# A four-layer decoder trunk on one core: later OUT turns, even blocks first in the out projection, own banks for the last piece

## The chip, the cores and the metric

The kernel runs on one core of a Trainium2 chip. The metric is the device time of one execution in microseconds. A core has a matrix engine (PE, TensorE), a vector engine (DVE), a scalar engine (ACT), a general engine (POOL) and a queue engine (SP) that issues most of the DMAs. Each engine runs its own program in order and waits for the others by semaphores. PE writes its products into PSUM, eight banks of 128 x 512 floats; DVE and ACT read them from there.

## The reference, cut to what matters

Four layers work on one residual stream of 256 tokens by 1024 features. Each layer is a token mixer and a squared-ReLU MLP, both behind an RMS norm. Mixer 0 (layers 0 and 3) is differential attention, mixer 1 (layer 1) block-sparse attention, mixer 2 (layer 2) sliding-window attention with sinks.

```python
def rms_norm(x, g):
    return x * rsqrt(mean(x * x, -1) + 1e-6) * g

def diff_attention(h, w_in, w_out, lam, sub_g, cos, sin, lambda_init):   # 8 heads, two maps each
    q, k, v = split(h @ w_in)                  # 1024 each; rotary on the first quarter of each head
    p = softmax(causal(q @ k.T / 8))
    p = p[:, :, 0] - lam * p[:, :, 1]
    o = rms_norm(p @ v, sub_g) * (1.0 - lambda_init)
    return o.reshape(B, S, 1024) @ w_out

for i in range(4):
    a = rms_norm(h, attn_norm_g[i])
    h = h + (diff_attention, moba_attention, swa_sink_attention)[i % 3](a, ...)
    a = maximum(rms_norm(h, mlp_norm_g[i]) @ mlp_w_up[i], 0)      # 1024 x 4096
    h = h + (a * a) @ mlp_w_down[i]                               # 4096 x 1024
return rms_norm(h, final_norm_g)
```

## The kernel before, in words

All is float32. A product is made of rounded parts: each operand x is split into hi, x rounded to a shorter float that PE takes at full rate, and lo, the rest. `mm3` (lines 271 to 273) sums hi·hi, hi·lo and lo·hi; `block_step` (603, 604) does the same for tokens in the free dimension, with hi and lo of the tokens side by side in one 512-wide matmul and one 256-wide one.

**Weights.** They lie in DRAM as 128 x 2048 pieces in the order of use. `fetch` loads a piece into one of four raw buffers; `stage` (lines 80, 81) splits it in two halves of 1024 columns, `whi` on ACT and `wlo` on DVE, into one of three buffers each. `take` hands out the next piece and, before that, has the pieces up to two ahead staged. With three buffers, the piece two ahead takes the buffer of the piece last used, so its first `whi` waits until PE has done the last matmul that reads it.

**The residual stream** stands transposed in four tiles `hT0` to `hT3`, each with two blocks of 128 features by 256 tokens. `into` (line 622) adds the eviction of block d to its half of `hT`, and then calls `norm_part`, which makes the scaled hi and lo of the block for the next projection (`hg`, line 228 on ACT and 229 on DVE), and for each second block the squares for the norm (233, 238).

**A differential layer.** `proj` (296) computes six pieces of q, k and v, 512 columns each, and between them calls turns from a written `plan`: `QK` transposes q and k of a pair of heads (`p_qk`, 459), `SC` scores and softmax (`p_s`, 271 to 273), `TR` transposes the weights (`p_t`, 351, evicted as `et`, 352), `AV` multiplies by v (`p_av`, 357 to 359) and makes the normed output `o` of a pair of heads (404), and `OUT` transposes it (`p_o`, 409) and evicts hi and lo as `oo` (411, 412). `OUT(g)` yields the two heads of pair g, which group g of the out projection reads as `parts[2g]` and `parts[2g+1]`. Evicted projections are `qk` (586), followed by the rotary sums (304 to 309).

**The out projection.** `out_proj_all` (layers 0, 2, 3) keeps four PSUM banks `p_d0` to `p_d3`, two blocks of 256 columns in each. For each of four groups it takes one weight piece and adds, for the eight blocks in order, two heads by `mm3`: 48 matmuls per group. In the last group each block goes through `into` as soon as it is done. `out_proj` does layer 1.

**The MLP.** `up_proj` has 16 groups of two blocks; in the first group its eight steps run over both blocks together, so step k needs only `hg` of block k. In layer 3 a callback after the second group transposes the residual back to rows (`p_res`, 797). `down_proj` returns to the transposed stream; in the last layer `down_out` computes rows instead, in two pieces of 512 columns for each of two groups of 128 rows: `last` accumulates in a bank `p_last`, `close` adds the residual (`res`, 702) and squares it (704), `sofar` and `finish` make the norm's factor (710 to 717), scale the rows (719, 722) and write them out. The very last piece is done in two halves of 256 columns.

**Start.** `WARM` products of two 128 x 128 tiles (line 133, 2 passes each) run while the first data comes in.

The order of calls is not the order of each engine's program: a scheduler places the instructions of every engine when the kernel is built, and from then on each engine takes them in that order.

Of the kernel before, what the change touches and what calls it, by code (L numbers as in the profile page):

```python
# [11 lines left out]
F32 = mybir.dt.float32  # L12
F32R = mybir.dt.float32r
I32 = mybir.dt.int32
AF = mybir.ActivationFunctionType
OP = mybir.AluOpType
AX = mybir.AxisListType

P = 128
# [8 lines left out]
NEG = -1.0e38  # L28
LOOK = 2
FAR = 5  # L30
WARM = 11
RAW = 4


# [5 lines left out]
def trunk(ctx: ExitStack, tc: tile.TileContext, xT, gains, lams, swa_row, fng, weights, out):  # L40
# [8 lines left out]
    def bank(tag, name):  # L49
        return ps.tile([P, 512], F32, tag=tag, name=name, bufs=4)  # L50
# [427 lines left out]
    def mixer_layer(i, n):  # L478
        mixer, slot = i % 3, i // 3
        r = norm_factor(n)  # L480
        parts = []
# [43 lines left out]
        else:  # L525
# [43 lines left out]
                    [(TR, 4), (QK, 3), (OUT, 1), (SC, 6)], [(TR, 5), (SC, 7)],  # L569
                    [(AV, 4), (TR, 6), (AV, 5), (TR, 7), (AV, 6), (OUT, 2), (AV, 7), (OUT, 3)]]  # L570
            if mixer == 0:
                plan[8:] = [[(AV, 2), (QK, 2), (OUT, 0), (SC, 4)], [(AV, 3), (SC, 5)], [(TR, 4), (AV, 4), (OUT, 1)],
                            [(TR, 5), (AV, 5)],
                            [(QK, 3), (SC, 6), (SC, 7), (OUT, 2), (TR, 6), (AV, 6), (TR, 7), (AV, 7), (OUT, 3)]]
            for at, c in enumerate(order):
                p = proj(n, (512, 2), at == 0, [lambda do=do, x=x: do(x) for do, x in plan[2 * at]])
                if i == 0 and at == 0:
# [11 lines left out]
                    do(x)  # L589
            for do, x in plan[-1]:  # L590
                do(x)
            return parts
        for do in first + second:
            do()
        for _ in range(3):
            step()
        line.clear()
        return parts

# [22 lines left out]
        if b:  # L624
            norm_sum(n, j)

    def out_proj_all(parts, n):

        banks = [bank("acc", f"p_d{j}") for j in range(4)]
        for g in range(4):  # L630
            hi, lo = (r3(2)(x) for x in take())
            for d in range(8):
                p = banks[d // 2][:, S * (d % 2):S * (d % 2) + S]
                w = slice(P * d, P * d + P)
                for a in range(2):
                    x = parts[2 * g + a]
                    mm3(p, hi[:, a, w], lo[:, a, w], x[:, 0], x[:, 1], g + a + d % 2 == 0, g + a == 4,
                        skip_group_check=True)
                if g == 3:
                    into(n, d, p, None, True)  # L640

    def out_proj(parts, n):

        banks = [bank("acc", f"p_d{j}") for j in range(4)]
        two = [[r3(4)(x) for x in take()] for _ in range(2)]
        order = [(k, d) for k in range(6) for d in range(4)] + [(k, d) for d in range(4) for k in (6, 7)]
        for k, d in order:
            hi, lo = (x[:, k % 4, P * d:P * d + P] for x in two[k // 4])
            block_step(banks[d], hi, lo, parts[k], k == 0, k == 7)
            if k == 7:  # L650
                into(n, d, banks[d], None)
        for j in range(2):
            hi, lo = (r3(8)(x) for x in take())
            for b in range(2):
                p = bank("acc", f"p_e{b}")
                for k in range(8):
                    block_step(p, hi[:, k, P * b:P * b + P], lo[:, k, P * b:P * b + P], parts[k], k == 0, k == 7)
                into(n, 4 + 2 * j + b, p, None)
# [32 lines left out]
    def down_out(us, res, factor):  # L691

        grow = sb.tile([P, D], F32, tag="raw", name="grow", bufs=RAW)
        nc.sync.dma_start(grow, bcast(fng, D))
        ss = cst.tile([P, 4, NT], F32, name="fss")
        x = cst.tile([P, 2, NT], F32, name="fx")
        r = cst.tile([P, NT], F32, name="fr")

        def close(t, bank, c, part, first, width):

            y = res[t][:, 512 * c + first:512 * c + first + width]
            V.scalar_tensor_tensor(y, bank[:, first:first + width], factor[:, t:t + 1], y, op0=OP.mult, op1=OP.add)
            sq = sb.tile([P, 512], F32, tag="relu", name="sq")
            A.activation(sq[:, :width], y, AF.Square, accum_out=ss[:, part, t:t + 1])

        def finish(t, halves):

            o = slice(t, t + 1)
            last = x[:, 1, o]
            V.scalar_tensor_tensor(last, ss[:, halves, o], 0.5 / D, x[:, 0, o], op0=OP.mult, op1=OP.add)  # L710
            y, w = r[:, o], tiny.tile([P, 1], F32, tag="nw", name="nw", bufs=6)

            V.tensor_scalar(y.bitcast(I32), last.bitcast(I32), -0.5, 1597463007.0 - 2.0 ** 22 - 2.0 ** 31,
                            op0=OP.mult, op1=OP.add)
            for _ in range(3):
                V.scalar_tensor_tensor(w, y, y, last, op0=OP.mult, op1=OP.mult)
                V.scalar_tensor_tensor(y, w, 1.5, y, op0=OP.subtract, op1=OP.mult)
            rows = slice(P * t, P * t + P)
            A.activation(res[t][:, :512], res[t][:, :512], AF.Copy, scale=y)
            nc.scalar.dma_start(out[rows, :512], res[t][:, :512])  # L720
            for z in (slice(512, 768), slice(768, 1024)):
                V.scalar_tensor_tensor(res[t][:, z], res[t][:, z], y, grow[:, z], op0=OP.mult, op1=OP.mult)
                nc.sync.dma_start(out[rows, z], res[t][:, z])

        def sofar(t, parts):
            o = slice(t, t + 1)
            V.tensor_scalar(x[:, 0, o], ss[:, 0, o], 0.5 / D, 0.5 * EPS, op0=OP.mult, op1=OP.add)
            for j in parts:
                V.scalar_tensor_tensor(x[:, 0, o], ss[:, j, o], 0.5 / D, x[:, 0, o], op0=OP.mult, op1=OP.add)

        for c in range(2):
            banks = [bank("acc", "p_last") for _ in range(NT)]
            parts = []

            def last(t, ks, cols=slice(0, 512)):
                for q, k in ks:
                    hi, lo = parts[q]
                    u, s = us[4 * q + k], slice(P * t, P * t + P)
                    mm3(banks[t][:, cols], u[:, 0, s], u[:, 1, s], hi[:, k, cols], lo[:, k, cols],
                        q + k == 0, q + k == 10, skip_group_check=True)  # L740

            for q in range(8):
                parts.append([r3(4)(x) for x in take()])
                if q < 6:
                    for k in range(4):
                        for t in range(NT):
                            last(t, [(q, k)])
            ends = [(q, k) for q in (6, 7) for k in range(4)]
            last(0, ends)
            close(0, banks[0], c, c, 0, 512)  # L750
            if c == 0:
                last(1, ends)
                close(1, banks[1], 0, 0, 0, 512)
                for t in range(NT):
                    y = res[t][:, :512]
                    V.tensor_tensor(y, y, grow[:, :512], op=OP.mult)
                    sofar(t, [])
            else:
                finish(0, 1)
                last(1, ends[:4])  # L760
                for h in range(2):
                    last(1, ends[4:], slice(256 * h, 256 * h + 256))
                    close(1, banks[1], 1, 1 + h, 256 * h, 256)
                    if h == 0:
                        sofar(1, [1])
                finish(1, 2)
# [7 lines left out]
    for j in range(4):  # L774
        norm_sum(n, j)
    for i in range(DEPTH):
        parts = mixer_layer(i, n)
        n = new_norm(gv[:, 1, i, :])
        (out_proj if i % 3 == 1 else out_proj_all)(parts, n)
        held = {}  # L780

        def then(g):
            if i + 1 < DEPTH:
                if g == 1:
                    x = mean_row(n)
                    held["row"] = sb.tile([P, S], F32, tag="row", name="row", bufs=1)
                    V.reciprocal(held["row"], x)
            elif g == 1:
                held["factor"] = cst.tile([P, NT], F32, name="factor")
                V.reciprocal(held["factor"], mean_square(n))  # L790

                held["res"] = [room(16 + t, [P, D], f"res{t}") for t in range(NT)]
                for j in range(4):
                    p = bank("acc", "p_res")
                    for t in range(NT):
                        for b in range(2):
                            T.transpose(p[:, S * t + P * b:S * t + P * b + P],
                                        hT[j][:, S * b + P * t:S * b + P * t + P], ident)
                    for t in range(NT):
                        A.activation(held["res"][t][:, S * j:S * j + S], p[:, S * t:S * t + S], AF.Copy)  # L800

        us = up_proj(n, then)
        if i + 1 < DEPTH:
            n = new_norm(gv[:, 0, i + 1, :])
            down_proj(us, n, held["row"])
        else:
            down_out(us, held["res"], held["factor"])
# [78 lines left out]
```

## Time and profile before

| | us |
|---|---|
| median of 3 runs | 1155.39 (1154.45 to 1156.26) |
| profiled execution, its time | 1154.87 |
| its span | 1152.8 |
| PE busy | 1140.4 (99%) |
| DVE busy | 824.3 (72%) |
| ACT busy | 671.6 (58%) |

The span runs from the first to the last instruction of the profiled execution. In the timeline a row gives start, duration, engine, line, operation, output and inputs, shapes and count, and in brackets how long the engine was idle before and what released it. Matmuls overlap, so the distance from one start to the next is what one costs on PE; a matmul's own duration is longer. The waits are listed as total, times and longest.

### The profile page before, as it was taken

To read this page: it belongs to the slowest core of one execution; us is meant where nothing else is said; L and a number is where in the kernel's file an instruction comes from. 1 tells how busy PE (TensorE), PEld (TensorE's weight loads), DVE (VectorE), ACT (ScalarE), POOL (GpSimd) and SP (SyncE) were. 2 spreads that over 40 slices of the span, in tenths; PEclk is the share of its full clock that TensorE was granted. 3 is DMA by queue.
4 is the path that set the end of the run, shared out by engine and by line. 5 is a ranking of instruction groups with operands and counts; after the bars stand their busy time and mean duration, and the time that the engine had idled before them with its cause. 6 is when DMAs were issued, how large, how long until landed. Compare 5 with 4: busy or idle time off the path is not lost.

```text
span 1152.8 us, 17102 instructions
## 1 busy us (share of the span) xinstructions
PE 1140.4 (99%) x6558; PEld 986.6 (86%) x6558; DVE 824.3 (72%) x1631; ACT 671.6 (58%) x1239; POOL 11.4 (1%) x39
## 2 busy tenths in 40 slices
PE   9999999999999999999999999999999999999997
PEld 7789888888887888888898888888888889888886
DVE  8978977656666698775568787775567788777453
ACT  6866655544476765654447866654447676665342
POOL 1000000000000000000000000000000000000000
PEclk9999999999999999999999999999999999999999
DMA  8543455555544355555564246555553434554551
GB/s 327 194 146 119 160 200 193 199 190 183 183 146 145 116 178 193 200 192 183 185 209 142 74 147 206 195 184 186 184 201 129 152 136 155 194 199 166 186 179 36
DMA packets 30608, 198.66 MB, mean 172 GB/s; under 512 B 3520, under 2 KB 5184, under 8 KB 7360
## 3 DMA queue, kind: packets, MB, share of 16 engines
q1 hardware_dynamic: 30240, 197.06, 49.6%
q8 instruction: 51, 0.84, 0.3%
q10 hardware_dynamic: 288, 0.52, 0.1%
q14 instruction: 29, 0.24, 0.1%
HBM read 196.52 MB, written 1.05 MB: 171 GB/s over the span
## 4 chain that ended last, share of the span: by engine, by line
PE 92%; DVE 3%; ACT 2%; DMA 2%; issue 1%; SPq 0%; DVEq 0%; ACTq 0%
PE p_up L603 20%; PE p_in L296 16%; PE p_down L603 15%; PE p_up L604 10%; PE p_down L604 8%; PE p_last L271 2%; PE p_last L273 2%; PE p_last L272 2%; PE p_d L273 2%; PE p_d L271 2%; DMA raw<-in_weights 2%; PE p_d L272 2%; PE p_av L434 1%; PE p_t L351 1%; PE p_s L271 1%; PE p_qk L459 1%
## 5 line engine op out<-in xcount | busy, mean ns | idle before, releaser
L81 DVE TENSOR_TENSOR wlo<-raw,whi 128x1024 fp32r<-128x1024 f32 (+1 forms) x374 | 447.1, 1209 | 202.9 <-ACT whi L80 201.9
L80 ACT ACTIVATE whi<-raw 128x1024 fp32r<-128x1024 f32 (+1 forms) x374 | 384.7, 1045 | 210.1 <-issue 111.1
L603 PE MATMUL p_up<-hg,whi 128*128 128x512 f32 x1024 | 356.9, 393 | 0.5 <-DVE hg L229 0.2
L604 PE MATMUL p_up<-hg,wlo 128*128 128x256 f32 x1024 | 284.9, 279 | 0.0
L603 PE MATMUL p_down<-uu,whi 128*128 128x512 f32 x768 | 266.4, 392 | 0.0
L603 PEld LDWEIGHTS p_up<-hg,whi 128*128 128x128 f32 x1024 | 191.5, 187 | 43.3 <-DVE hg L229 0.7
L604 PE MATMUL p_down<-uu,wlo 128*128 128x256 f32 x768 | 214.3, 279 | 0.0
L296 PE MATMUL p_in<-whi,hg 128*128 128x512 f32 (+1 forms) x736 | 212.9, 372 | 0.1
L604 PEld LDWEIGHTS p_up<-hg,wlo 128*128 128x128 f32 x1024 | 193.2, 189 | 0.5
L603 PEld LDWEIGHTS p_down<-uu,whi 128*128 128x128 f32 x768 | 143.7, 187 | 32.1
L296 PEld LDWEIGHTS p_in<-whi,hg 128*128 128x128 f32 x736 | 131.8, 188 | 24.7 <-issue 1.2
L604 PEld LDWEIGHTS p_down<-uu,wlo 128*128 128x128 f32 x768 | 144.8, 189 | 0.0
L296 PE MATMUL p_in<-wlo,hg 128*128 128x512 f32 (+1 forms) x368 | 130.3, 368 | 0.1
L676 ACT ACTIVATE uu<-u 128x512 fp32r<-128x512 f32 x64 | 40.5, 633 | 70.9 <-DVE u L674 70.9
L296 PEld LDWEIGHTS p_in<-wlo,hg 128*128 128x128 f32 x368 | 68.8, 188 | 12.1 <-DVE wlo L81 1.3
L609 ACT ACTIVATE cross<-p_up 128x256 f32<-128x256 f32 x128 | 48.1, 376 | 39.4 <-PE p_up L604 34.0
L228 ACT ACTIVATE hg<-hT,gn 128x256 fp32r<-128x256 f32 x64 | 31.6, 503 | 65.6 <-DVE hT L622 65.1
L336 ACT ACTIVATE e<-ns,nm 128x128 f32<-128x128 f32 (+1 forms) x128 | 56.8, 447 | 10.3 <-DVE nm L333 10.0
L677 DVE TENSOR_TENSOR uu<-u,uu 128x512 fp32r<-128x512 f32 x64 | 44.2, 691 | 21.5 <-ACT uu L676 21.5
L271 PE MATMUL p_d<-oo,whi 128*128 128x256 f32 x192 | 56.2, 293 | 0.0
L272 PE MATMUL p_d<-oo,whi 128*128 128x256 f32 x192 | 55.1, 287 | 0.0
L273 PE MATMUL p_d<-oo,wlo 128*128 128x256 f32 x192 | 54.7, 288 | 0.0
(182 smaller groups left out, 1262.1 us busy)
## 6 DMA issues: line engine op xcount, KB each, us to landing
raw<-in_weights SPq DMA_DIRECT2D x181, 1024.0 KB, 4.8
raw<-in_weights SPq DMA_DIRECT2D x8, 256.0 KB, 4.6
raw<-in_weights SPq DMA_DIRECT2D x4, 512.0 KB, 7.6
hT<-in_xT SPq DMA_DIRECT2D x8, 128.0 KB, 4.5
bias<-in_swa_row SPq DMA_DIRECT2D x1, 512.0 KB, 3.6
grow<-in_fng SPq DMA_DIRECT2D x1, 512.0 KB, 3.5
out<-res SPq DMA_DIRECT2D x4, 128.0 KB, 2.1
out<-res ACTq DMA_DIRECT2D x2, 256.0 KB, 2.2
```

Of the source, the lines that this page charges most:

```text
L80: A.activation(hi[:, s], raw[:, s], AF.Copy)
L81: V.tensor_tensor(lo[:, s], raw[:, s], f(hi[:, s]), op=OP.subtract)
L271: T.matmul(out, lh, rh, start=start, stop=False, **kw)
L272: T.matmul(out, lh, rl, start=False, stop=False, **kw)
L273: T.matmul(out, ll, rh, start=False, stop=stop, **kw)
L296: T.matmul(out[t], n.both[k // 2][:, k % 2, x, P * t:P * t + P], r3(kb)(parts[k // kb][w])[:, k % kb, :], start=fresh, stop=k == 7 and x + ...
L336: A.activation(e[:, s], ns[:, s], AF.Exp, bias=nm[:, t:t + 1], scale=-1.0, accum_out=l[:, t:t + 1])
L603: T.matmul(r3(2)(p), hi, x, start=start, stop=False, skip_group_check=True)
L604: T.matmul(p[:, :S], lo, x[:, 0], start=False, stop=stop, skip_group_check=True)
L609: A.activation(cross, p[:, S:], AF.Copy)
L676: A.activation(both[:, :, 0], r3(2)(u), AF.Copy)
L677: V.tensor_tensor(both[:, :, 1], r3(2)(u), f(both[:, :, 0]), op=OP.subtract)
```

## The change

Four edits:

1. `WARM` goes from 11 to 12.
2. In the plan of a differential layer, `OUT(1)` moves from the middle of the sixth projection (the last turn called there) to behind it (the first turn called there). `OUT(3)` leaves the plan; `mixer_layer` returns it as a function that `out_proj_all` calls in group 2 ahead of block 1.
3. `out_proj_all` goes over the blocks in the order 0, 2, 4, 6, 1, 3, 5, 7 in every group.
4. In the last piece of `down_out`, all but the last four of its 32 steps are closed by a 512-wide `res` without squares, and each half of the last four steps accumulates in a bank of its own and is added by its own `close`.

```diff
-WARM = 11
+WARM = 12
...
             if mixer == 0:
-                plan[8:] = [[(AV, 2), (QK, 2), (OUT, 0), (SC, 4)], [(AV, 3), (SC, 5)], [(TR, 4), (AV, 4), (OUT, 1)],
-                            [(TR, 5), (AV, 5)],
-                            [(QK, 3), (SC, 6), (SC, 7), (OUT, 2), (TR, 6), (AV, 6), (TR, 7), (AV, 7), (OUT, 3)]]
+                plan[8:] = [[(AV, 2), (QK, 2), (OUT, 0), (SC, 4)], [(AV, 3), (SC, 5)], [(TR, 4), (AV, 4)],
+                            [(OUT, 1), (TR, 5), (AV, 5)],
+                            [(QK, 3), (SC, 6), (SC, 7), (OUT, 2), (TR, 6), (AV, 6), (TR, 7), (AV, 7)]]
...
-            return parts
+            return parts, (lambda: OUT(3))
...
-        return parts
+        return parts, lambda: None
...
-    def out_proj_all(parts, n):
+    def out_proj_all(parts, n, rest):
...
-            for d in range(8):
+            for d in (0, 2, 4, 6, 1, 3, 5, 7):
+                if (g, d) == (2, 1):
+                    rest()
...
-    def out_proj(parts, n):
+    def out_proj(parts, n, rest):
...
-        def close(t, bank, c, part, first, width):
-
+        def close(t, p, c, part, first=0):
+
+            width = p.shape[-1]
             y = res[t][:, 512 * c + first:512 * c + first + width]
-            V.scalar_tensor_tensor(y, bank[:, first:first + width], factor[:, t:t + 1], y, op0=OP.mult, op1=OP.add)
-            sq = sb.tile([P, 512], F32, tag="relu", name="sq")
-            A.activation(sq[:, :width], y, AF.Square, accum_out=ss[:, part, t:t + 1])
+            V.scalar_tensor_tensor(y, p, factor[:, t:t + 1], y, op0=OP.mult, op1=OP.add)
+            if part is not None:
+                sq = sb.tile([P, 512], F32, tag="relu", name="sq")
+                A.activation(sq[:, :width], y, AF.Square, accum_out=ss[:, part, t:t + 1])
...
-            def last(t, ks, cols=slice(0, 512)):
+            def last(t, ks, p=None, first=0, alone=False):
+                p = banks[t] if p is None else p
+                cols = slice(first, first + p.shape[-1])
                 for q, k in ks:
                     hi, lo = parts[q]
                     u, s = us[4 * q + k], slice(P * t, P * t + P)
-                    mm3(banks[t][:, cols], u[:, 0, s], u[:, 1, s], hi[:, k, cols], lo[:, k, cols],
-                        q + k == 0, q + k == 10, skip_group_check=True)
+                    mm3(p, u[:, 0, s], u[:, 1, s], hi[:, k, cols], lo[:, k, cols],
+                        (q, k) == (ks[0] if alone else (0, 0)), (q, k) == ks[-1] and k == 3 and q > 5,
+                        skip_group_check=True)
...
-            close(0, banks[0], c, c, 0, 512)
+            close(0, banks[0], c, c)
...
                 finish(0, 1)
+
                 last(1, ends[:4])
+                close(1, banks[1], 1, None)
                 for h in range(2):
-                    last(1, ends[4:], slice(256 * h, 256 * h + 256))
-                    close(1, banks[1], 1, 1 + h, 256 * h, 256)
+                    p = bank("acc", "p_last")[:, :256]
+                    last(1, ends[4:], p, 256 * h, True)
+                    close(1, p, 1, 1 + h, 256 * h)
                     if h == 0:
                         sofar(1, [1])
                 finish(1, 2)
...
-        parts = mixer_layer(i, n)
+        parts, rest = mixer_layer(i, n)
         n = new_norm(gv[:, 1, i, :])
-        (out_proj if i % 3 == 1 else out_proj_all)(parts, n)
+        (out_proj if i % 3 == 1 else out_proj_all)(parts, n, rest)
```

More of the change, by code (lines that the diff above doesn't have):

```diff
@@ L749, in down_out @@
             last(0, ends)
-            close(0, banks[0], c, c, 0, 512)
+            close(0, banks[0], c, c)
             if c == 0:
                 last(1, ends)
-                close(1, banks[1], 0, 0, 0, 512)
+                close(1, banks[1], 0, 0)
                 for t in range(NT):
```

## The prediction

> **What bounds the kernel now.** I read the page first (span, busy shares, the chain), then the waits of the matrix engine, then the timeline of each place that the diff touches, engine by engine.
>
> ```profile
> span 1152.8 us, 17102 instructions
> PE 1140.4 (99%) x6558; PEld 986.6 (86%) x6558; DVE 824.3 (72%) x1631; ACT 671.6 (58%) x1239; POOL 11.4 (1%) x39
> PE 92%; DVE 3%; ACT 2%; DMA 2%; issue 1%; SPq 0%; DVEq 0%; ACTq 0%
> ...
> PE p_o L409 <- DVE o L404: 1.5, 4, 0.5
> PE p_last L271 <- DVE res L702: 0.6, 1, 0.6
> PE p_up L603 <- DVE hg L229: 0.2, 1, 0.2
> ```
>
> TensorE works 1140.4 of 1152.8 us and carries 92% of the chain. The matmuls stay the same in number and size, apart from one warming product, so the change can only close holes in PE's stream or open new ones. The waits (total, times, longest) name the holes aimed at: p_o (the OUT turns of the two differential layers) and p_last (end); p_up after the out projection is a small one. A wait is shorter than the loss, since the modelled matmul ends overlap the hole, so I price holes from start to start.
>
> **Warming product: 0.**
>
> ```profile
> 1.00 4.58 PE L133 MATMUL p_warm<-ones 128*128 128x128 f32 x22 [1.00 <-POOL ones L124]
> 5.68 1.22 PE L296 MATMUL p_in<-whi,hg 128*128 128x512 f32 x3
> 6.12 0.63 ACT L80 ACTIVATE whi<-raw 128x512 fp32r<-128x512 f32 x1 [0.50 <-DMA raw<-in_weights]
> ```
>
> Eleven products are 22 passes in 4.58 us, 0.21 each, ending at 5.58. A twelfth adds 0.2 to 0.4. What hides it is the DMA: the first p_in waits for its operands until 5.68, and the next quarter of the weight begins to be rounded only at 6.12, when its DMA has landed. Without that cover it would cost at most 0.4; I keep that for the range and take 0.
>
> **OUT(1), behind the last projection: -0.35 in each of layers 0 and 3.**
>
> ```profile
> 84.45 0.39 PE L296 MATMUL p_in<-wlo,hg 128*128 128x512 f32 x1
> 85.08 0.63 PE L409 MATMUL p_o<-ident,o 128*128 128x128 f32 x4 [0.24 <-DVE o L404]
> 85.74 0.69 ACT L411 ACTIVATE oo<-p_o,gn 128x512 fp32r<-128x512 f32 x1 [1.28 <-PE p_o L409]
> 90.10 0.69 ACT L586 ACTIVATE qk<-p_in,nr 128x512 f32<-128x512 f32 x1 [0.72 <-PE p_in L296]
> 90.68 0.48 ACT L352 ACTIVATE et<-p_t 128x384 f32<-128x384 f32 x1
> 92.23 1.04 PE L459 MATMUL p_qk<-ident,qk 128*128 128x128 f32 x8
> ```
>
> p_o starts 0.63 after the matmul before it, where that one's pitch is 0.23: a hole of 0.40. In the new order p_o stands behind the last p_in, beside p_t, and its input is some 4 us old: the hole goes, and so do the switches between formats on either side. The gain is at most 0.87 (hole, four transposes and switches leave the projection; the transposes return). But p_o's evictions, 0.69 on ACT and about 0.75 on DVE, now stand between the qk eviction (90.10) and et (90.68), and ahead of the rotary sums on which p_qk (92.23) waits. These queues delay the second p_av and p_qk, so part of the lead is given back. Bounds 0.0 and 0.87; I take 0.35, near the hole, because p_d matmuls already stand there to fill. Two layers: -0.7.
>
> **OUT(3), inside the out projection: -0.60 in each of layers 0 and 3.**
>
> ```profile
> 109.98 0.28 PE L272 MATMUL p_d<-oo,whi 128*128 128x256 f32 x1
> 110.78 0.63 PE L409 MATMUL p_o<-ident,o 128*128 128x128 f32 x4 [0.52 <-DVE o L404]
> 112.95 0.74 DVE L412 SCALAR_TENSOR_TENSOR oo<-p_o,gn,oo 128x512 fp32r<-128x512 f32 x1
> 116.47 2.01 ACT L80 ACTIVATE whi<-raw 128x1024 fp32r<-128x1024 f32 x2 [4.31 <-PE p_d L272]
> ```
>
> Start to start 0.80, where a p_d follows the one before after 0.12: 0.68 at most; I take 0.60, since the change to the transposes' format stays. Now p_o stands before block 1 of group 2, 19 p_d later (19 x 0.12 = 2.3), long after o is ready. What is late next is oo, the operand of group 3: DVE ends it at about 114.5 instead of 113.7, and group 3 begins at about 115.8 (116.47, where the last read of the weight before it frees a buffer, less the gain). Slack over 1 us; without it the wait would come back. Two layers: -1.2.
>
> **Out projection, even blocks first: +2.05 in layers 0 and 2, +0.4 in layer 3.** This is the part that decides.
>
> ```profile
> 124.42 1.05 ACT L80 ACTIVATE whi<-raw 128x1024 fp32r<-128x1024 f32 x1
> 117.31 0.42 DVE L622 TENSOR_TENSOR hT<-p_d,hT 128x256 f32<-128x256 f32 x1 [3.62 <-PE p_d L273]
> 117.65 2.35 DVE L81 TENSOR_TENSOR wlo<-raw,whi 128x1024 fp32r<-128x1024 f32 x2
> 119.92 0.48 DVE L229 SCALAR_TENSOR_TENSOR hg<-hT,gn,hg 128x256 fp32r<-128x256 f32 x1
> 120.32 1.08 DVE L622 TENSOR_TENSOR hT<-p_d,hT 128x256 f32<-128x256 f32 x3
> 125.89 1.21 DVE L81 TENSOR_TENSOR wlo<-raw,whi 128x1024 fp32r<-128x1024 f32 x1
> ...
> 120.45 0.50 PE L603 MATMUL p_up<-hg,whi 128*128 128x512 f32 x1
> 120.79 0.28 PE L604 MATMUL p_up<-hg,wlo 128*128 128x256 f32 x1
> 120.91 0.40 PE L603 MATMUL p_up<-hg,whi 128*128 128x512 f32 x1
> 121.15 0.28 PE L604 MATMUL p_up<-hg,wlo 128*128 128x256 f32 x1
> 123.42 0.28 PE L272 MATMUL p_d<-oo,whi 128*128 128x256 f32 x1
> 123.54 0.28 PE L273 MATMUL p_d<-oo,wlo 128*128 128x256 f32 x1
> ```
>
> The second block of a bank need no longer wait until the first has been read, but that saves nothing: p_up waits for hg of block 0, which stands behind the two wlo on DVE (117.65 to 120.0, then 119.92 + 0.48 = 120.40), and starts at 120.45 either way.
>
> What is lost comes from the order of the programs. Now ACT and DVE finish block 1 early (among the three hT at 120.32 and the hg behind them), and the next weight's whi (124.42) and wlo (125.89) come near the end. In the changed program ACT's order is hg of blocks 0, 2, 4, 6, then the first half of the next whi, then hg of block 1; DVE's is all eight hT, the first half of that wlo, then hg of block 1. That whi takes the buffer that group 3 reads, so it waits for PE's last L272 of block 7. Behind it in both queues stands hg of block 1, which the second step of p_up needs. In the times of layer 0:
>
> - p_up starts at 120.45; after three of its matmuls (0.34, 0.12, 0.24 by the rows) blocks 3, 5, 7 start at 121.15: 18 p_d at 0.12, to 123.31.
> - The last L272 is the 17th: 123.07, done 123.35. whi 123.39 to 124.44 (1.05), wlo 124.46 with 1.14 to the next, hg of block 1 125.60 to 126.08; p_up can go on at 126.13.
> - PE has between them only five p_up matmuls of the first step, of this group and the next: 3 x 0.12 + 2 x 0.24 = 0.83, to 124.14.
>
> The hole is 126.13 - 124.14 = 1.99, and the first matmul behind a hole takes 0.34 instead of 0.24: about 2.05. The bounds: 1.8 if each handover is 0.1 quicker, 2.3 if DVE takes wlo's whole 1.21 and starts late. Nothing in these programs can move ahead of that queue.
>
> ```profile
> 671.83 0.47 PE L603 MATMUL p_up<-hg,whi 128*128 128x512 f32 x1 [0.22 <-DVE hg L229]
> 977.92 1.91 PE L797 MATMUL p_res<-ident,hT 128*128 128x128 f32 x16
> ```
>
> Layer 2 has the same programs here (671.83 answers to 120.45): 2.05 again. In layer 3 the 16 transposes of the residual move from 977.92 into the hole and fill about 1.66 of it (at 0.104 each): 0.4 is left. Layer 1 uses the other function. Sum: +4.5.
>
> By the row the clock stands through a hole of the present kind:
>
> ```profile
> 28.00:31.00 3.00, 2.34 (x11) 1.64 (x11) 2.73 (x8) 3.00 (x6) 0.00 (x0) 1.00 0.21 87
> ```
>
> PE was idle for 0.66 of these 3 us (busy 2.34) and the granted clock is 1.00. The Trainium skill, "TensorE: Matmul & The Clock Gate" (section "HAM oscillation — how this bites in real kernels"), has the gate closing only for idle gaps over about 3.4 us; by it a 2 us hole costs no more than itself, so the sum stays. No trace here has so long a hole.
>
> **End: -0.8.**
>
> ```profile
> 1139.17 0.75 DVE L702 SCALAR_TENSOR_TENSOR res<-p_last,factor,res 128x512 f32<-128x512 f32 x1 [7.43 <-PE p_last L273]
> 1143.00 0.28 PE L273 MATMUL p_last<-whi,uu 128*128 128x256 f32 x1
> 1143.32 0.48 DVE L702 SCALAR_TENSOR_TENSOR res<-p_last,factor,res 128x256 f32<-128x256 f32 x1
> 1143.85 0.39 PE L271 MATMUL p_last<-whi,uu 128*128 128x256 f32 x1 [0.58 <-DVE res L702]
> 1145.58 0.48 DVE L702 SCALAR_TENSOR_TENSOR res<-p_last,factor,res 128x256 f32<-128x256 f32 x1 [1.05 <-PE p_last L273]
> ```
>
> The second half of the last piece waits until the first half of the same bank is read: 0.85 start to start against 0.12, plus 0.10 of restart. With banks of its own it ends 0.82 earlier, at about 1144.76. The price is one more 512-wide res on DVE (0.75, as at 1139.17). It falls at about 1142.2 into the first rows' finishing, pushes that to about 1144.5, and DVE is free just before the last product. Bounds +0.3 (DVE late) and -0.84; I take -0.8.
>
> **Sum.** -0.7 - 1.2 - 0.8 + 4.5 = +1.8. The profiled execution took 1154.87 for a span of 1152.8, so it would become 1156.7; the median 1155.39 is 0.5 above it, so 1157.2 is forecast for the median. About 0.2% (2.3 us) is what a measurement of this kernel can tell from no change.
>
> **The rivals.**
> - A, the holes do not appear: hg of block 1 is ready by 124.14. For it: hT of block 1 is written by about 122.6. Against: ACT and DVE take their queues in order, and whi stands ahead. Gains alone: 1155.39 - 2.7 = 1152.7, faster. Chance 0.12.
> - B, the moved evictions of OUT(1) take the place of its wait: ACT's 0.69 and DVE's 0.75 in front of p_qk eat the lead. It decides where p_qk of the last pair starts no earlier than 92.23. Then -0.7 is gone (1157.9), and where the evictions last longer than the lead the turn costs up to 0.4 in each layer: 1158.7, slower. For it: both engines have next to no idle time from 90.10 to 92.2. Against: p_d fills PE. Chance 0.25.
> - C, the clock falls in the two holes of 2 us: 22 cold passes took 0.21 each against 0.104 in p_res, 2.3 us lost per warming: 1157.2 + 4.6 = 1161.8. Chance 0.05.
> - D, the turns land where they were and nothing moves: 1155.4. Chance 0.03.
>
> **How the numbers follow.** The forecast has 0.55, its own range 1156.0 to 1158.6 (gains 2.0 to 3.3, holes 4.1 to 5.0 and the spread of runs). Of it 0.40 lies within 0.2% (up to 1157.7) and 0.15 above. A gives 0.10 faster and 0.02 same; B 0.20 slower, 0.05 same; C 0.05 slower; D 0.03 same. Faster 0.10, same 0.50, slower 0.40. The range 1152.6 to 1160.0 takes in A and B and leaves C out.
>
> **What would show it.** p_o and p_last gone from PE's waits; in their place p_up L603 <- DVE hg L229 with about 2 us twice; whi, wlo, hg one behind the other just before each; p_res at about 967 instead of 978 in layer 3. The forecast is wrong if PE runs on past the fifth p_up, or if those holes are below 1 us.

## The result, and the profile after

The changed kernel took 1157.97 us in the median of 13 runs against 1154.66 for the kernel before (13 runs beside them): a ratio of 1.0023, 95% interval 1.0015 to 1.0031, or 2.7 us slower (1.7 to 3.6); the two medians stand 3.3 apart. The forecast was +1.8. The 13 times of the kernel before lie between 1154.38 and 1156.26, those of the changed one between 1155.98 and 1159.52: it is not only slower, it scatters more.

The page of the changed kernel, its first lines and the chain, and then PE's waits (total us, times, longest):

```profile
span 1156.2 us, 17102 instructions
PE 1141.2 (99%) x6560; PEld 984.9 (85%) x6560; DVE 825.7 (71%) x1632; ACT 671.2 (58%) x1239; POOL 11.4 (1%) x39
...
PE 95%; DVE 2%; ACT 1%; issue 1%; DMA 0%; SPq 0%; DVEq 0%
...
PE p_up L603 <- DVE hg L229: 4.7, 5, 1.9
PE p_qk L459 <- DVE qk L309: 0.7, 1, 0.7
PE p_in L296 <- ACT hg L228: 0.4, 1, 0.4
```

Both waits that the change aims at, p_o (1.5) and p_last (0.6), are gone. p_up's has grown from 0.2 to 4.7 us. The timeline of layer 0 at the end of the out projection shows its making, ACT first, then DVE, then PE:

```profile
119.87 1.31 ACT L228 ACTIVATE hg<-hT,gn 128x256 fp32r<-128x256 f32 x3 [1.89 <-DVE hT L622]
122.48 1.06 ACT L80 ACTIVATE whi<-raw 128x1024 fp32r<-128x1024 f32 x1 [1.30 <-PE p_d L272]
123.45 0.49 ACT L228 ACTIVATE hg<-hT,gn 128x256 fp32r<-128x256 f32 x1
...
121.62 1.41 DVE L622 TENSOR_TENSOR hT<-p_d,hT 128x256 f32<-128x256 f32 x4
123.57 1.23 DVE L81 TENSOR_TENSOR wlo<-raw,whi 128x1024 fp32r<-128x1024 f32 x1 [0.55 <-ACT whi L80]
124.72 0.88 DVE L229 SCALAR_TENSOR_TENSOR hg<-hT,gn,hg 128x256 fp32r<-128x256 f32 x2
...
122.28 0.28 PE L273 MATMUL p_d<-oo,wlo 128*128 128x256 f32 x1
123.11 0.28 PE L604 MATMUL p_up<-hg,wlo 128*128 128x256 f32 x1
125.25 0.50 PE L603 MATMUL p_up<-hg,whi 128*128 128x512 f32 x1 [1.86 <-DVE hg L229]
```

ACT is idle for 1.30 us in front of whi, until PE's last read (L272) of the weight that held the buffer; hT of block 1, which its next instruction scales, was first of the four written from 121.62. DVE then waits 0.55 for whi, does wlo, and only then hg of block 1 (124.72). PE stops at 123.11 and goes on at 125.25: 2.14 from start to start. Layer 2 has the same row (678.72, idle 1.86), and in layer 3 the 16 p_res (the transposes of the residual) now fill the place:

```profile
678.72 0.50 PE L603 MATMUL p_up<-hg,whi 128*128 128x512 f32 x1 [1.86 <-DVE hg L229]
...
969.99 1.91 PE L807 MATMUL p_res<-ident,hT 128*128 128x128 f32 x16
972.00 0.50 PE L603 MATMUL p_up<-hg,whi 128*128 128x512 f32 x1
```

Where the time went is read by pairing each matmul of one profile with the same one of the other and taking the difference of their starts. After minus before, in us:

| place | shift there | change |
|---|---|---|
| second half of the first projection (26 us) | +0.30 | +0.30, start |
| p_qk of the last pair, layer 0 (92) | -0.09 | -0.33 from the shift of +0.24 at 74 us, OUT(1) |
| first p_up, layer 0 (120) | -0.89 | -0.80, OUT(3) |
| after the hole, layer 0 | +1.31 | +2.20 |
| after the hole, layer 2 (700) | +3.45 | +2.23 (from +1.22 at the first p_up, 672) |
| p_qk of the last pair, layer 3 (936) | +3.15 | -0.30, OUT(1) |
| behind the transition, layer 3 (981) | +2.80 | OUT(3) -0.81, transition +0.47 |
| end of that up projection (1057) | +4.26 | +1.46 |
| last matmul | +3.46 | -0.82, own banks |

The -0.80 in front of the first p_up of layer 0 is not OUT(3)'s alone. In the changed kernel four p_d run ahead of the last pair's p_qk, where three did before, so 0.12 of it (the pitch of one p_d) was won at OUT(1), and 0.68, the whole hole, at OUT(3).

Two lines are on no list of the prediction: the start, and the +1.46 that builds up evenly over the whole up projection of layer 3. There a pair of matmuls (512 and 256 wide) takes 353 ns instead of 347, with no wait. The windows (us, busy time and count of PE, PEld, DVE, ACT, POOL, granted clock, DMA share, GB/s) show it as 115 matmuls in 20 us instead of 118, at a clock of 1.00; the first row is of the changed kernel, the second of the kernel before:

```profile
1000.00:1020.00 20.00, 20.00 (x115) 17.36 (x114) 15.43 (x21) 12.03 (x19) 0.00 (x0) 1.00 0.56 196
```

```profile
997.00:1017.00 20.00, 20.00 (x118) 17.62 (x117) 15.83 (x22) 11.96 (x19) 0.00 (x0) 1.00 0.55 195
```

### The profile page after: what moved, and what is told of

Same layout as the page of the kernel before. It is cut to its first block, busy times and chain, and to the rows that moved or that the text cites. A ratio compares the mean times of both kernels' runs of the same rounds, so it can differ in the third digit from the quotient of the medians.

```text
span 1156.2 us, 17102 instructions
## 1 busy us (share of the span) xinstructions
PE 1141.2 (99%) x6560; PEld 984.9 (85%) x6560; DVE 825.7 (71%) x1632; ACT 671.2 (58%) x1239; POOL 11.4 (1%) x39
## 4 chain that ended last, share of the span: by engine, by line
PE 95%; DVE 2%; ACT 1%; issue 1%; DMA 0%; SPq 0%; DVEq 0%
PE p_up L603 21%; PE p_in L296 18%; PE p_down L603 15%; PE p_up L604 10%; PE p_down L604 8%; PE p_last L271 3%; PE p_last L272 3%; PE p_last L273 3%; PE p_d L273 2%; PE p_d L271 2%; PE p_d L272 2%; DVE wlo L81 1%; PE p_t L351 1%; PE p_av L434 1%; PE p_s L271 1%; PE p_qk L459 1%
## 5 line engine op out<-in xcount | busy, mean ns | idle before, releaser
L272 PE MATMUL p_d<-oo,whi 128*128 128x256 f32 x192 | 55.2, 288 | 0.0
```

Source lines behind the costliest of these rows:

```text
L272: T.matmul(out, lh, rl, start=False, stop=False, **kw)
```

## The experiments

Ratios are to the kernel before, run beside each experiment on the same chip: e1 to e4 on one chip, e5 to e8 on another.

**e1: the order of blocks undone, all else kept.**

```diff
-            for d in (0, 2, 4, 6, 1, 3, 5, 7):
-                if (g, d) == (2, 1):
+            for d in range(8):
+                if (g, d) == (2, 4):
                     rest()
```

> The changed kernel with the out projection's blocks back in the order 0 to 7 in all groups, and OUT(3) called at the same place in group 2 (behind four blocks); the other three edits stay. Theory (hg of block 1 queued behind the next weight's rounding makes the holes): the waits p_up L603 <- DVE hg of about 1.9 us are gone, what is left are the gains measured between the two traces, 0.33 + 0.80 in layer 0, 0.30 + 0.81 in layer 3, 0.82 at the end, less 0.3 at the start: 2.5 to 3.1 us below the kernel before. Rival (the moved turns or the last piece's banks cost the time): it stays slower than the kernel before by 1 us or more.

Measured: 1152.05 us against 1154.88, ratio 0.9975 (0.9965 to 0.9984), 2.8 us faster, the nine times within 0.7 us. Its waits:

```profile
PE p_qk L459 <- DVE qk L309: 0.7, 1, 0.7
PE p_s L271 <- issue: 0.6, 1, 0.6
PE p_up L603 <- DVE hg L229: 0.2, 1, 0.2
```

p_up's wait is back at the 0.2 of the kernel before, and p_o's and p_last's stay away. The rival, that the moved turns cost the time, falls.

**e2: the kernel before with the order of blocks alone.**

```diff
-            for d in range(8):
+            for d in (0, 2, 4, 6, 1, 3, 5, 7):
```

> The kernel before with only the block order changed, even blocks first in all groups. Theory: holes of 2.20 (layer 0) and 2.27 (layer 2) at the second step of p_up and 0.5 in layer 3 come alone: 4.9 us above the kernel before, more where an up projection runs at the longer pitch (353 ns for a pair of matmuls instead of 347, 1.6 us a stage). Rival (the order costs only together with the moved OUT(3), whose evictions crowd the same queues): less than 2 us above the kernel before.

Measured: 1160.9 against 1154.88, ratio 1.0058 (1.0044 to 1.0072), 6.0 us slower; five times from 1160.23 to 1162.6. The waits of p_up are those of the changed kernel, so the order needs no help from the moved turns:

```profile
PE p_up L603 <- DVE hg L229: 4.7, 5, 1.9
PE p_o L409 <- DVE o L404: 1.5, 4, 0.5
PE p_last L271 <- DVE res L702: 0.6, 1, 0.6
```

From its shifts the three transitions cost 2.04, 2.22 and 0.50: 4.8 us. The profile, of the execution of 1160.23, has the loads of the start 0.8 us later as well, and with these its 5.4 us are accounted for. The median execution of 1160.9 has a mean granted clock of 0.999, as the kernel before, so a fall of the clock (shown in e4) is not in its 6.0; the rest of them, 0.4 if its start was as late, was not traced.

**e3: another order without neighbours in a bank, block 1 third.**

```diff
-            for d in (0, 2, 4, 6, 1, 3, 5, 7):
-                if (g, d) == (2, 1):
+            for d in (0, 2, 1, 4, 3, 6, 5, 7):
+                if (g, d) == (2, 3):
```

> The changed kernel with the blocks in the order 0, 2, 1, 4, 3, 6, 5, 7: still no block directly behind the other of its bank, but block 1 third. ACT now has hg of blocks 0, 2, 1, 4, 3, 6 ahead of the next weight's whi and only those of 5 and 7 behind it, and PE has about 3.0 us of steps and second-group matmuls between the last block and the step that needs block 5. Theory: no wait of p_up above 0.6 us, time as with the order 0 to 7, 2.5 to 3.1 us below the kernel before. Rival (what costs is to leave the bank's second block for later, whichever block stands behind the rounding): a hole of about 1 us or more at the step of block 5 and a time at or above that of the kernel before.

Measured: 1152.28, ratio 0.9977 (0.9969 to 0.9986), 2.6 us faster than the kernel before and level with e1. ACT of this kernel in layer 0:

```profile
121.42 0.97 ACT L228 ACTIVATE hg<-hT,gn 128x256 fp32r<-128x256 f32 x2
122.30 0.62 ACT L233 ACTIVATE sq<-hT 128x512 f32<-128x512 f32 x1
122.82 0.49 ACT L228 ACTIVATE hg<-hT,gn 128x256 fp32r<-128x256 f32 x1
123.87 2.01 ACT L80 ACTIVATE whi<-raw 128x1024 fp32r<-128x1024 f32 x2 [0.56 <-PE p_d L272]
125.79 0.49 ACT L228 ACTIVATE hg<-hT,gn 128x256 fp32r<-128x256 f32 x1
```

whi again stands in front of two hg and waits for PE again, but these are of blocks 5 and 7, and PE has 3 us of other steps before it needs them. Leaving a bank's second block for later costs little: by the shifts the three transitions come to 0.47 us, and the median stands 0.23 above that of e1. What costs is which block stands behind the wait.

**e4: the changed kernel again.**

> The changed kernel unchanged, a second profile and more times. Theory (an up projection falls into one of two pitches when its stream starts after a wait): times in groups some 1.7 us apart, lowest near 1.5 us above the kernel before; this profile shows pairs of p_up matmuls at 353 ns in another set of layers than layer 3 alone, or in none. Rival (layer 3's 353 ns belongs to the program, for instance to the moved p_res): layer 3 alone has 353 ns again, and the times spread no more than those of the kernel before.

Measured: five times, 1157.08, 1159.29, 1159.38, 1160.66 and 1161.32; ratio 1.0041 (1.0028 to 1.0053). In this profile layer 3 runs at 347 ns a pair, so the 353 belongs to an execution and not to the program. But something else shows, in layer 0 behind the hole. The windows:

```profile
124.20:126.40 2.20, 0.36 (x3) 0.03 (x1) 1.66 (x3) 2.20 (x5) 0.00 (x0) 1.00 0.09 37
126.40:127.40 1.00, 0.98 (x5) 0.89 (x6) 1.00 (x3) 1.00 (x4) 0.00 (x0) 1.00 0.00 0
127.40:130.80 3.40, 3.40 (x13) 2.88 (x12) 3.12 (x5) 1.93 (x3) 0.00 (x0) 0.52 0.11 17
130.80:134.00 3.20, 3.20 (x19) 2.81 (x19) 1.00 (x3) 1.18 (x2) 0.00 (x0) 0.97 0.83 315
```

and three rows of the timeline there:

```profile
127.59 0.63 PE L603 MATMUL p_up<-hg,whi 128*128 128x512 f32 x1
128.02 0.42 PE L604 MATMUL p_up<-hg,wlo 128*128 128x256 f32 x1
128.23 0.63 PE L603 MATMUL p_up<-hg,whi 128*128 128x512 f32 x1
```

About a microsecond after PE restarts, the granted clock falls to half for 3.4 us (the clock column: (3.40 x 0.48 + 3.20 x 0.03) / 0.5 = 3.5), and a pair takes 0.64 us instead of 0.35. Five pairs and a bit: 1.6 us lost beyond the hole itself. The Trainium skill, "TensorE: Matmul & The Clock Gate" (section "HAM oscillation — how this bites in real kernels"), sets the limit at idle gaps over about 3.4 us; this gap was 2.14 from start to start, so here the measurement decides. The same page of the Trainium skill, in its Part 1, calls the window of the gate free-running; that would explain why only some executions are hit, and the traces agree (end of e6). The expected groups 1.7 apart did not come out cleanly: falls of the clock, the longer pitch and the start's loads (+1.4 us at 26 us in this profile) lie over each other.

**e5 and e6: a shorter and a longer hole.** e5 rounds the one weight piece that stands in the way in four parts instead of two; e6 puts two copies on DVE in front of lo of block 1.

```diff
+        w = 512 if i in (18, 107, 155) else w
         for h in range(2048 // w):
```

> The changed kernel, with the one weight piece that stands between the blocks (the third of the up projection, in layers 0, 2 and 3) rounded in four parts of 512 columns instead of two of 1024. The orders stay, but ahead of hg of block 1 stands now one part of 512 on ACT (0.63 instead of 1.05 us) and, on DVE, none. Theory of the queue: the start-to-start hole at the second step of p_up falls from 2.14 to about 0.9 us in layers 0 and 2 and goes in layer 3. Theory of the clock (a hole of 2.1 us lets the gate close for one period of 3.4 us in about 4 of 10 cases, since it then fills most of one period of a free-running window; one of 1 us never does): the granted clock is 1.0 throughout in every execution, the times lie within about 1 us of each other, and the median is 1.0 to 1.5 us below the kernel before. Rival (the clock falls at the restart after any wait, or the spread comes from the start's loads): spread of 3 us as for the changed kernel.

```diff
-        V.scalar_tensor_tensor(both[:, 1], h, g, f(both[:, 0]), op0=OP.mult, op1=OP.subtract)
+        hi = f(both[:, 0])
+        for _ in range(2 if d == 1 and len(staged) in (18, 107, 155) else 0):
+            late = sb.tile([P, S], F32, tag="y", name="late")
+            V.tensor_copy(late, hi)
+            hi = late
+        V.scalar_tensor_tensor(both[:, 1], h, g, hi, op0=OP.mult, op1=OP.subtract)
```

> The changed kernel, with two copies of 128 x 256 on DVE put in front of lo of block 1 (same three pieces): behind the wlo of the next weight come two copies, lo of block 3 and a sum of squares, and only then lo of block 1. Theory of the queue: the hole grows from 2.14 by about 1.6 to some 3.7 us start to start in layers 0 and 2, and by as much in layer 3. Theory of the clock: with 3.6 us idle the gate closes after nearly every one of these holes, two of them or more in most executions, 1.6 us each; the mean granted clock of the executions is 0.996 to 0.997 and the median some 9 us above the kernel before. Rival (the falls of the clock are chance and have nothing to do with the length): no more than one fall in an execution on average, the median about 6.5 to 8 us above.

e5 measured: 1154.13, ratio 0.9993 (0.9984 to 1.0001); eleven times from 1153.68 to 1154.39. The restart in layer 0, first of e5, then of e6:

```profile
122.96 0.28 PE L605 MATMUL p_up<-hg,wlo 128*128 128x256 f32 x1
123.94 0.50 PE L604 MATMUL p_up<-hg,whi 128*128 128x512 f32 x1 [0.70 <-DVE hg L230]
```

```profile
123.05 0.28 PE L609 MATMUL p_up<-hg,wlo 128*128 128x256 f32 x1
126.69 0.47 PE L608 MATMUL p_up<-hg,whi 128*128 128x512 f32 x1 [3.35 <-DVE hg L234]
```

The hole follows what stands in front of hg: 0.98 in e5 (expected 0.9), 3.63 in e6 (expected 3.7). With the short one the scatter is gone, 0.7 us over eleven runs, and no execution's clock is below 0.998, as the theory of the clock has it. The median is 0.75 below the kernel before where 1.0 to 1.5 was expected, and the interval does not tell it from no change; in layer 3, where the hole was expected to go, the transition still costs 0.28 by the shifts. e6 measured 1164.09, ratio 1.008 (1.0066 to 1.0094), 9.2 us slower (expected 9). The mean granted clock is 0.995 or 0.996 in each of its five executions, where the kernel before has 0.998 or 0.999. Its windows in layers 0 and 2:

```profile
123.00:126.70 3.70, 0.35 (x3) 0.05 (x2) 3.18 (x7) 3.70 (x8) 0.00 (x0) 1.00 0.03 13
126.70:130.50 3.80, 3.80 (x14) 3.22 (x15) 3.48 (x6) 1.41 (x3) 0.00 (x0) 0.62 0.28 47
130.50:132.00 1.50, 1.50 (x9) 1.31 (x8) 0.00 (x0) 0.00 (x0) 0.00 (x0) 0.83 0.96 404
679.50:683.20 3.70, 0.35 (x3) 0.08 (x1) 3.22 (x7) 3.70 (x8) 0.00 (x0) 1.00 0.02 7
683.20:687.50 4.30, 4.30 (x16) 3.69 (x17) 3.45 (x6) 1.37 (x3) 0.00 (x0) 0.60 0.31 91
687.50:690.00 2.50, 2.50 (x16) 2.18 (x15) 0.06 (x1) 0.47 (x2) 0.00 (x0) 1.00 0.62 262
```

Behind both holes the clock is at half, each time for 3.4 us ((3.80 x 0.38 + 1.50 x 0.17) / 0.5 and 4.30 x 0.40 / 0.5). So the fall goes with the length of the hole: none in any profile behind 1 us, behind one of the six of 2.14 in the profiles of the changed kernel, e2 and e4, behind both of 3.6.

What decides at 2.1 us can be read from the traces. Between the first and the last change of the clock that a trace records, every stretch at one clock is a whole number of 3.413 us: 122.88 is 36 of them, 1024.00 is 300, 552.96 is 162. So the clock is set anew at fixed periods of 3.413 us, and the question is how much of one period PE is idle. The period with the hole and the one behind it, first in layer 0 of e4, then in layer 0 of e2:

```profile
124.14:127.55 3.41, 1.55 (x9) 1.08 (x8) 2.86 (x6) 3.41 (x8) 0.00 (x0) 1.00 0.06 24
127.55:130.97 3.42, 3.42 (x13) 2.94 (x12) 3.12 (x5) 1.78 (x3) 0.00 (x0) 0.50 0.16 24
```

```profile
123.42:126.83 3.41, 1.63 (x12) 1.26 (x10) 2.86 (x7) 2.69 (x5) 0.00 (x0) 1.00 0.44 185
126.83:130.24 3.41, 3.33 (x19) 2.94 (x20) 3.24 (x7) 3.00 (x6) 0.00 (x0) 1.00 0.00 0
```

In e4 the idle 1.86 us lie in one period (3.41 - 1.55) and the clock falls; in e2 a little of the hole lies in the next period, 1.78 is left, and it stands. Over all periods of the ten profiles, from the first recorded change on, the clock fell behind each with 1.86 us or more of PE idle and behind none with 1.78 or less. The hole is 2.14 in all these profiles; where a period begins differs from one to the next.

**e7: e1 with eleven warming products.**

```diff
-WARM = 12
+WARM = 11
```

> The kernel with the order 0 to 7 and the other edits, but eleven warming products instead of twelve. Theory (the start is set by the loads, and the 0.3 us at the start of the two profiles is their scatter): the same time as with twelve, within 0.3 us. Rival (the twelfth product delays the first projection): 0.3 us or more below it, and the first projections of this profile no later than in the kernel before.

Measured: 1151.97, ratio 0.9976 (0.9966 to 0.9985), against 1152.05 and 0.9975 for e1: no difference that this can tell. At 26 us its profile stands at -0.23 and e1's at +0.32, but e2, with eleven too, stands at +0.80: the loads at the start scatter by more than a warming product costs.

**e8: e3 with the wlo in front of hg of block 0 in four parts.**

```diff
+        w = 512 if i in (17, 106, 154) else w
         for h in range(2048 // w):
```

> The kernel with the blocks in the order 0, 2, 1, 4, 3, 6, 5, 7 and the other edits, and the piece whose wlo stands in front of hg of block 0 (the second of the up projection in layers 0, 2 and 3) rounded in four parts of 512 columns. Theory: DVE can begin this wlo half a microsecond earlier, so hg of block 0 and with it the first p_up come up to 0.3 us earlier in each of the three layers: 0 to 0.9 us below the same kernel without it. Rival (four parts cost DVE and ACT their fixed time, about 0.1 us each, and the three hT that now stand in front of hg of block 0 eat the lead): no faster, up to 0.6 us above.

Measured: 1153.03, ratio 0.9985 (0.9976 to 0.9994): not faster than e3, which was expected to be beaten by up to 0.9. The median is 0.75 above e3's, but on another chip, and the two intervals overlap. DVE, and then PE, in layer 0:

```profile
115.86 2.49 DVE L82 TENSOR_TENSOR wlo<-raw,whi 128x512 fp32r<-128x512 f32 x4 [1.95 <-ACT whi L81]
118.27 1.07 DVE L623 TENSOR_TENSOR hT<-p_d,hT 128x256 f32<-128x256 f32 x3
...
118.74 0.39 PE L272 MATMUL p_d<-oo,whi 128*128 128x256 f32 x1 [0.59 <-DVE hT L623]
```

With shorter parts the scheduler put all four in front of the first hT, where in e3 one hT (116.63) comes ahead of them. The second block of a bank now waits for that eviction; PE stands 0.87 from start to start in each of the three layers. By the shifts the three transitions cost 0.73 us, where e3's cost 0.47. A part made shorter changed the order, and the new order took away what the part had given.

## Why the prediction was right, and where it was not

**What decides: right.** The step "whi waits for PE's last L272, and hg of block 1 stands behind it in both queues" came out as written: hole 2.14 from start to start (forecast 1.99 beyond a pitch of 0.12, so 2.11), 2.20 and 2.23 lost by the shifts in layers 0 and 2 (forecast 2.05), p_res in the third one with 0.47 left (0.4). e1, e2 and e5 show that the order alone makes it and that it goes with what stands in front of hg.

**The gains: right.** OUT(1) gave 0.45 in layer 0, the 0.33 of the table and the p_d of 0.12 that ran early (forecast 0.35). OUT(3) gave 0.68 there (0.60, too small: in the new place the p_d in front of p_o keeps its pitch of 0.12, so that the whole hole of 0.68 went, and I had held some of it back for the change of format). Layer 3 agrees to 0.03, and the last piece gave 0.82 (0.8). Together 3.1, and e1 as a whole 2.8 against the forecast 2.7. Rival B falls with e1, and by its own sign: p_qk of the last pair starts at 92.15, not later than 92.23, although this profile began 0.30 late.

**The warming product: right within what can be told** (e7).

**What failed is the sentence that the clock stands through a hole of the present kind, so that "a 2 us hole costs no more than itself".** It was read off a row with 0.66 us of idle and a rule, and no row showed 2 us. Rival C had this mechanism, with a chance of 0.05 and a price of 2.3 us for each of two holes. The runs show 1.6 us, in some executions and not always at both holes.

The mean granted clocks of the 13 executions of the changed kernel say in which; one fall takes 1.7 of some 1157 us, 0.0015, off such a mean. The five that took 1155.98 to 1156.92 all have 0.999, so no fall: their median is 1.4 above that of the kernel before, near the forecast of +1.8. Of the other eight, 1157.69 to 1159.52, six have 0.996 or 0.997, which none of the 44 executions of the kernel before beside the experiments has (0.998 or 0.999): these had a fall. Two have 0.998, which leaves it open; one of them is the profiled one, with no fall and the longer pitch in its place. The median execution, 1157.97 at 0.997, is one of the six. So what lies between the forecast and the median is in the main this term, which the prediction put at nothing.

**That the median lies in the range is in part luck.** The forecast of 1157.2 started from 1155.39, the median of three runs; thirteen gave 1154.66. From there the same sum would have given 1156.5, and a range from 1155.3 to 1157.9, just short of the 1157.97 measured. A base 0.7 too high made up for some of what the falls added.

**What stays open** is what sets the pitch of 353 ns in one up projection of the first profile. e6 has it in the same layer (115 matmuls between 1020 and 1040 us), e4, e2 and e5 do not; all of these have p_up starting on a wait there, so the wait does not bring it. In e6 the stream even runs at 347 for 10 us behind its last wait (979.39) and changes to 353 near 989.5, with no wait there. Nor was it tried how the time divides between falls and pitch in executions without a profile.

The version that beats both is e1, or e7 with eleven products: 1152.0 us, 2.8 to 2.9 below the kernel before and about 6 below the changed one.

## What to carry to other kernels

When a loop is reordered so that one engine need not wait, look at the programs of the engines behind it: a producer that was done early may now stand behind an instruction that waits for the end of the very loop that was reordered. Ask of each in-order queue what the first instruction that can block waits for, and whether anything behind it is needed sooner. And a hole of some 2 us in TensorE's stream can cost more than its length: here 1.6 us more whenever 1.86 us or more of idle fell into one of the clock's periods of 3.413 us.

## What the runs showed of the hardware

The granted clock fell to half for 3.4 us about 1 us after the restart from holes of 2.14 us (in e4's profile in layer 0, not in layer 2, and in neither layer in those of the changed kernel and of e2) and of 3.63 us (both layers of e6); it did not fall behind 0.98 us (e5). Its changes lie whole multiples of 3.413 us apart, and it fell behind every such period with 1.86 us or more of PE idle and behind none with 1.78 or less, in ten profiles. A stream of alternating 512- and 256-wide matmuls with equal instructions ran at 347 ns a pair in nearly every up and down projection and at 353 in layer 3's up projection of the first profile, for 76 us on end at a granted clock of 1.00, and in most of the same projection in e6.
